# Tables asked for after the first weights, and 144 modulation steps spread anew over two mixers and two gate builds

## The chip, the cores and the metric

The kernel runs on one core of one Trainium2 chip. The metric is the device time of one execution in microseconds; where several executions are told of, it is their median.

## What is computed

Two blocks of a transformer run one after the other on 256 tokens of width 1024, each with two layers. The first block has a mixer and a PEER layer per layer; the second is steered by a condition `c` and has two feed-forward layers and a mixer per layer. Cut to what matters here:

```python
x = x + hgrn_gmlp_mixer(x, ...)          # mix0
x = x + peer_ffn(x, ...)                 # peer0
x = x + mla_moba_mixer(x, ...)           # mix1
x = x + peer_ffn(x, ...)                 # peer1

def peer_ffn(x, norm_ffn, w_query, sub_keys, expert_down, expert_up):
    # top 16 of 128x128 experts for each token and each of 8 heads
    act = gelu(einsum('btd,bthkd->bthk', xi, take(expert_down, idx)))
    return einsum('bthk,bthkd->btd', g * act, take(expert_up, idx))

def adaln(cond, w, b):                   # once per layer of the second block,
    mm = jax.nn.silu(cond) @ w + b       # for c and for c_ctx
    return nine rows of 1024             # w is 1024 x 9216

x = x + 0.5 * m[2] * swiglu(modulate(x, g, m[0], m[1]), ffn1_wi, ffn1_wo)
x = x + m[5] * mixer(modulate(x, g, m[3], m[4]))
x = x + 0.5 * m[8] * swiglu(modulate(x, g, m[6], m[7]), ffn2_wi, ffn2_wo)
```

The modulation (`adaln`) depends on the condition alone. It can be computed at any time before the second block begins.

## The kernel before, in words

Activations lie transposed, 128 features by 256 tokens to a tile. A product with weights is made of three matmuls (`mm3`, lines 170 to 172): weights and activations are each split into a rounded part and a rest (`whi` and `wlo`, `xnh` and `xnl`), and high by high, high by low and low by high are added up. Weights come in units of 512 KB (128x1024, fp32). For each unit SP issues a DMA (`raw`, line 85), ACT casts it (`whi`, line 93), and DVE or POOL subtracts the cast from it (`wlo`, line 97). All stages share three slots for `raw`.

The stages run in this order: `mix0` (`hgrn_gmlp`), `peer0`, `mix1` (`mla_moba`), `peer1`, then the second block. In a mixer, an input projection is followed by the heads' own work (scores at line 408, the gMLP product at line 443, head norms `hps` and `hrb` at lines 287 and 296) and by an output projection into `acc`. A PEER layer begins with a norm (`nps`, line 226) and the routing: 16 units of `l_wq`, each followed by a score product with `keys` (line 530, keys issued at line 513). Then come the *gate build* and the expert products. In the build, one-hot tables for four tokens at a time are made by DVE and ACT, and PE multiplies them into `gps` (line 641), while the down products of the first 46 experts (`dn`) are spread among them. Behind the build come the other downs, with the up products (`acc`).

A *modulation step* (`Mod.step`, line 931) loads 512 KB of `w_mod` (`mraw`, line 937) and multiplies it by the condition in four column-tiled fp32 matmuls (line 942). Eight steps make a row. The eighth copies the row out of PSUM (`mrow`, line 946), two transposes turn it (line 948), and two DVE additions write it away (line 952). There are 72 steps to a layer, 144 in all.

Where the steps stand is set by three numbers and a scheduler. In a mixer they are given out ahead of it under `n.low()`, with a priority far behind the mixer's own work and a pool of their own of three slots. The scheduler puts them into each engine's program where it expects that engine to be free, but none may stay behind when the mixer ends, since the pools close there. In a PEER layer they are given out when the downs reach number 46 (line 670), from the `raw` slots that the weights use. The order in each engine's program is fixed when the kernel is built: 40 steps of layer 0 in the first mixer (`M_0`), 32 of layer 1 in the first build (`N_MOD`), the other 32 of layer 0 in the second mixer (`M_1`), and the last 40 of layer 1 in the second build.

At the start SP issues `vec`, the two halves of `x`, then `ident` and `iota` (lines 119 and 120), then the six tables of the first mixer (line 131), then the first three `raw` and the first three `mraw`.

Of the kernel before, what the change touches and what calls it, by code (L numbers as in the profile page):

```python
# [18 lines left out]
T = 256  # L19
# [2 lines left out]
NEG = -1.0e30  # L22
N_STORE = 40
N_LAG = 16
N_PARK = 3
N_MOD = 32
M_0 = 40
M_1 = 72
PAT_1 = "gggv"
PAT_0 = "gv"  # L30
M_BUFS = 3
# [69 lines left out]
class Net:  # L101
    def __init__(self, ctx, tc, d):
        self.ctx, self.tc, self.nc, self.d = ctx, tc, tc.nc, d
        nc = self.nc
        pool = lambda name, bufs, **k: ctx.enter_context(tc.tile_pool(name=name, bufs=bufs, **k))
        self.cp = pool("const", 1)
        self.main = Stream(self, ctx, "w", 3, 3)
        self.xn_p = None
        self.ps, self.bufs, self.rotation, self.turn = None, {}, [], 0
        self.x = self.cp.tile([128, NDC, T], F32, name="x")  # L110
        self.vec = self.cp.tile([128, NVEC], F32, name="vec")
        self.ident = self.cp.tile([128, 128], F32, name="ident")
        self.ones = self.cp.tile([128, 128], F32, name="ones")
        self.iota = self.cp.tile([128, 128], F32, name="iota")
        self.eps = self.cp.tile([128, 1], F32, name="eps")
        nc.sync.dma_start(out=self.vec, in_=d["vec"])
        for c in range(0, NDC, X_DMA):
            nc.sync.dma_start(out=self.x[:, c:c + X_DMA], in_=d["x_t"][:, c:c + X_DMA])
        nc.sync.dma_start(out=self.ident, in_=d["c_ident"])
        nc.sync.dma_start(out=self.iota, in_=d["c_iota"])  # L120
        nc.vector.memset(self.ones, 1.0)
        nc.vector.memset(self.eps, EPS)
        self.stream = self.main
# [181 lines left out]
def hgrn_gmlp(n: Net):  # L305
    nc, d = n.nc, n.d
    n.rotation = ["mm", "ac", "mm", "ac", "mm", "ac", "ac"]
    n.stream.pattern = PAT_0
    with ExitStack() as st:
        p = st.enter_context(n.tc.tile_pool(name="m0", bufs=1, reuse_waits="tile"))  # L310
        w2 = st.enter_context(n.tc.tile_pool(name="m0w", bufs=2, reuse_waits="tile"))
        xn, rn = n.scaled(n.x, n.v("l0_norm_mix"), None, None, p)
        rc = n.columns(rn, p)
        sel = n.const("c_sel", p, [128, 4, 128])
        lev = n.const("c_lev", p, [128, 6, 128])
        smask = n.const("c_scan", p, [128, T])
        tril = n.const("c_tril", p, [128, 128])
        gws = n.const("gmlp_ws", p, [128, 4, 128])
        gbs = n.const("gmlp_bs", p, [128, 4, 128])


        lb = n.v("lb").rearrange("p (r h) -> p r h", r=3)
# [41 lines left out]
        def tiles(kt, qt, dst):  # L364
# [9 lines left out]
            out=s, in0=ps, in1=n.ident.unsqueeze(1).to_broadcast([128, 4, 128]), op=OP.mult))  # L374
# [110 lines left out]

def peer(n: Net, layer, mod, mod_upto):
    nc, d = n.nc, n.d
    pre = f"l{layer}_"  # L490
    NS = N_STORE
# [1 line left out]
    with ExitStack() as st:  # L493
# [123 lines left out]
        with ExitStack() as sg:  # L617
            gp = sg.enter_context(n.tc.tile_pool(name="gg", bufs=1, reuse_waits="tile"))
            gg = gp.tile([128, 128 - NS, T], F32, name="gg")
            onehot = n.tc.tile_pool(name="oneh", bufs=OH, reuse_waits="tile")  # L620
            o2 = onehot.__enter__()
            for t0 in range(0, T, 4):
                a = o2.tile([128, 4, 128], F32, tag="oa", name="oa")
                b = o2.tile([128, 4, 128], F32, tag="ob", name="ob")
                g = n.bank("gps").rearrange("p (t e) -> p t e", t=4)


                by_act = t0 // 4 * N_ACT % 16 < N_ACT
                nc.vector.tensor_tensor(out=a, in0=n.iota.unsqueeze(1).to_broadcast([128, 4, 128]),
                                        in1=it[:, 0, t0:t0 + 4].unsqueeze(2).to_broadcast([128, 4, 128]),  # L630
                                        op=OP.is_equal)
                for t in range(4):
                    at = lambda s: it[:, s, t0 + t:t0 + t + 1]
                    if by_act:
                        nc.scalar.activation(out=b[:, t], in_=n.iota, func=AF.Abs, scale=-1.0, bias=at(1))
                        nc.scalar.activation(out=b[:, t], in_=b[:, t], func=AF.Relu, scale=-2.0, bias=at(2))
                    else:
                        nc.vector.tensor_scalar(out=b[:, t], in0=n.iota, scalar1=at(1), scalar2=at(2),
                                                op0=OP.is_equal, op1=OP.mult)
                for t in range(4):  # L640
                    nc.tensor.matmul(g[:, t], a[:, t], b[:, t], start=t == 0, stop=True, skip_group_check=True)  # L641
                ge = g.rearrange("p t e -> p e t")
                nc.vector.tensor_tensor(out=ca[:, :, t0:t0 + 4], in0=ca[:, :, t0:t0 + 4], in1=ge[:, 0:NS], op=OP.mult)
                nc.scalar.copy(out=gg[:, :, t0:t0 + 4], in_=ge[:, NS:128])
            n.stream.pattern = PAT_G
            onehot.__exit__(None, None, None)
            g2 = sg.enter_context(n.tc.tile_pool(name="gg2", bufs=2, reuse_waits="tile"))

            def coef(i):
                return ca[:, i] if i < NS else gg[:, i - NS]  # L650

            acc = []

            def up(i):
                if not acc:
                    acc.extend(n.accs())
                w = n.unit(d[pre + "up"][i])
                c = coef(i)
                ch = g2.tile([128, T], F32R, tag="ch", name="ch")
                cl = g2.tile([128, T], F32R, tag="cl", name="cl")  # L660
                n.split(c, ch, cl)
                n.up(acc, w, (ch, cl), i == 0, i == 127)

            done = 0
            for i in range(NS, 128, 2):
                def sink(b):
                    nc.scalar.activation(out=b, in_=b, func=AF.Gelu_apprx_tanh)
                    c = gg[:, i - NS:i - NS + 2]
                    nc.vector.tensor_tensor(out=c, in0=c, in1=b, op=OP.mult)
                if i == NS + 2 * N_PARK:  # L670
                    while mod.next < mod_upto:
                        mod.step(n.main.raw_p)
                    mod.bank = None
                down_pair(i, sink, "ac" if i < NS + 2 * N_PARK else None)
                while i >= NS + 2 * N_PARK and done < i + 2 - N_LAG:
                    up(done)
                    done += 1
            while done < 128:
                up(done)
                done += 1  # L680
            n.residual(n.x, acc)
# [779 lines left out]
def two_blocks_kernel(ctx: ExitStack, tc: tile.TileContext, d, out, stages=None):  # L1461
    stages = stages or STAGES
    n = Net(ctx, tc, d)
    nc = n.nc
# [9 lines left out]
    for s in stages:  # L1474
        with tc.tile_pool(name="xn", bufs=1, reuse_waits="tile") as n.xn_p:
# [4 lines left out]
                    (hgrn_gmlp if s == "mix0" else mla_moba)(n)  # L1480
            elif s.startswith("peer"):
                with n.psum(ac=4, mm=2, m2=2):
                    peer(n, int(s[4]), mods[1], N_MOD if s[4] == "0" else 72)
            elif s.startswith("mod"):
                with n.psum(ac=4, mm=2, fl=2), tc.tile_pool(name="mod", bufs=3, reuse_waits="tile") as p:
                    aside(mods[int(s[3])], p, 72)
# [172 lines left out]
```

## Time and profile before

| what | value |
|---|---|
| median of 3 runs | 3417.71 us (3415.21 to 3419.04) |
| the profiled execution | 3413.94 us |
| its span in the trace | 3412.1 us |
| mean granted clock of TensorE | 0.984 |
| first mixer | 0 to about 190 us |
| first gate build, first score to first up product | 198.2 to 483.4 us |
| second mixer, its last product | ends at 1246.4 us |
| second gate build, likewise | 1256.5 to 1557.7 us |

The span is the time from the first to the last instruction that the profiler recorded; the profiled execution took 1.84 us more. The places in the table are starts of instructions in the trace, in microseconds from the start of the span. What one edit is worth is read at such a place: which engine is waited for there, and what stands behind the wait in its program.

### The profile page before, as it was taken

How to read it: one execution, taken by the hardware profiler on the slowest of the kernel's cores; microseconds unless marked ns; L12 is line 12 of the kernel's file. 1: busy time of each engine (PE TensorE's matmuls, PEld its weight loads, DVE VectorE, ACT ScalarE, POOL GpSimd, SP SyncE). 2: the span in 40 equal slices, each digit the busy share in tenths (PEclk: the TensorE clock that was granted, in tenths of full speed). 3: DMA queues.
4: the chain of work that ended last, by engine and by line, in shares of the span. 5: the costliest groups of instructions: out<-in, count | busy, mean ns of one | idle time of the engine just before them, and what ended most of it. 6: DMA issues, size and time to landing. Idle time of an engine off the chain costs nothing.

```text
span 3412.1 us, 65304 instructions
## 1 busy us (share of the span) xinstructions
PE 3286.0 (96%) x26792; PEld 3139.3 (92%) x26792; DVE 2144.8 (63%) x4167; ACT 1684.6 (49%) x2720; POOL 169.5 (5%) x79
## 2 busy tenths in 40 slices
PE   7999999999999999999999999899999989999898
PEld 6789989999999679978999999899999779999898
DVE  6489785555556559785555555666766656666565
ACT  5444774444445344584544444544644444454543
POOL 2200000000001310000000000200000010100100
PEclk9999999999999999999999999999999889999999
DMA  6645465555555545456655555554454235455453
GB/s 229 231 159 180 150 222 182 202 185 181 184 183 193 193 144 169 161 200 208 201 183 185 182 184 183 202 184 138 155 172 148 77 124 185 168 179 173 143 185 106
DMA packets 165755, 598.28 MB, mean 175 GB/s; under 512 B 18512, under 2 KB 20176, under 8 KB 164944
## 3 DMA queue, kind: packets, MB, share of 16 engines
q1 hardware_dynamic: 165456, 594.11, 52.0%
q8 instruction: 210, 3.44, 0.4%
q14 instruction: 89, 0.73, 0.1%
HBM read 592.99 MB, written 1.05 MB: 174 GB/s over the span
## 4 chain that ended last, share of the span: by engine, by line
PE 86%; DVE 7%; DMA 3%; ACT 2%; issue 1%; SPq 0%; ACTq 0%; DVEq 0%
PE acc L170 11%; PE acc L171 11%; PE acc L172 10%; PE dn L172 7%; PE dn L171 7%; PE dn L170 7%; PE ff L170 6%; PE ff L171 6%; PE ff L172 6%; DMA mraw<-w_mod 2%; PE gps L641 2%; PE mm L170 2%; PE mm L171 2%; PE mm L172 2%; PE mod L942 2%; DVE wlo L97 2%
## 5 line engine op out<-in xcount | busy, mean ns | idle before, releaser
L93 ACT CAST whi<-raw 128x1024 fp32r<-128x1024 f32 x969 | 1014.0, 1048 | 1400.5 <-PE acc L171 533.2
L97 DVE TENSOR_TENSOR wlo<-raw,whi 128x1024 fp32r<-128x1024 f32 x904 | 1110.4, 1229 | 827.9 <-ACT whi L93 827.5
L172 PE MATMUL dn<-xnh,wlo 128*128 128x256 f32 x2048 | 581.2, 284 | 2.9 <-DVE wlo L97 2.9
L170 PE MATMUL dn<-xnh,whi 128*128 128x256 f32 x2048 | 581.1, 284 | 1.2 <-ACT whi L93 1.2
L171 PE MATMUL dn<-xnl,whi 128*128 128x256 f32 x2048 | 580.9, 284 | 0.0
L171 PE MATMUL acc<-cl,whi 128*128 128x256 f32 x2048 | 567.5, 283 | 1.0 <-DVE cl L165 1.0
L172 PE MATMUL acc<-ch,wlo 128*128 128x256 f32 x2048 | 566.4, 283 | 0.0
L170 PE MATMUL acc<-ch,whi 128*128 128x256 f32 x2048 | 533.8, 283 | 0.0
L170 PE MATMUL ff<-xnh,whi 128*128 128x258 f32 x1760 | 503.6, 287 | 12.5 <-DVE x L209 3.9
L171 PE MATMUL ff<-xnl,whi 128*128 128x258 f32 x1760 | 502.5, 286 | 3.7 <-DVE xnl L247 3.7
L172 PE MATMUL ff<-xnh,wlo 128*128 128x258 f32 x1760 | 500.4, 284 | 3.3 <-POOL wlo L97 1.9
L172 PEld LDWEIGHTS dn<-xnh,wlo 128*128 128x128 f32 x2048 | 393.1, 192 | 3.8 <-DVE wlo L97 3.8
L170 PEld LDWEIGHTS dn<-xnh,whi 128*128 128x128 f32 x2048 | 393.7, 192 | 1.6 <-ACT whi L93 1.6
L171 PEld LDWEIGHTS acc<-cl,whi 128*128 128x128 f32 x2048 | 393.2, 192 | 1.4 <-DVE cl L165 1.4
L171 PEld LDWEIGHTS dn<-xnl,whi 128*128 128x128 f32 x2048 | 393.6, 192 | 0.0
L172 PEld LDWEIGHTS acc<-ch,wlo 128*128 128x128 f32 x2048 | 392.7, 192 | 0.0
L170 PEld LDWEIGHTS acc<-ch,whi 128*128 128x128 f32 x2048 | 373.1, 192 | 0.0
L170 PEld LDWEIGHTS ff<-xnh,whi 128*128 128x128 f32 x1760 | 334.8, 191 | 16.7 <-ACT rstd L216 4.8
L171 PEld LDWEIGHTS ff<-xnl,whi 128*128 128x128 f32 x1760 | 336.8, 192 | 5.3 <-DVE xnl L247 4.6
L172 PEld LDWEIGHTS ff<-xnh,wlo 128*128 128x128 f32 x1760 | 335.4, 191 | 4.6 <-POOL wlo L97 2.5
L97 POOL TENSOR_TENSOR wlo<-raw,whi 128x1024 fp32r<-128x1024 f32 (+1 forms) x65 | 156.3, 2411 | 2754.4 <-ACT whi L93 2726.9
L171 PE MATMUL acc<-hl,whi 128*128 128x256 f32 x880 | 246.1, 281 | 3.1 <-DVE hl L1019 3.1
(449 smaller groups left out, 5315.6 us busy)
## 6 DMA issues: line engine op xcount, KB each, us to landing
raw<-l_down SPq DMA_DIRECT2D x256, 512.0 KB, 3.3
raw<-l_up SPq DMA_DIRECT2D x256, 512.0 KB, 4.2
mraw<-w_mod SPq DMA_DIRECT2D x144, 512.0 KB, 4.3
raw<-f1i SPq DMA_DIRECT2D x132, 512.0 KB, 3.3
raw<-f2i SPq DMA_DIRECT2D x88, 512.0 KB, 3.3
raw<-f1o SPq DMA_DIRECT2D x66, 512.0 KB, 3.3
raw<-w_t SPq DMA_DIRECT2D x46, 512.0 KB, 4.3
raw<-f2o SPq DMA_DIRECT2D x44, 512.0 KB, 3.4
```

The lines of the kernel that those rows point to most:

```text
L93: nc.scalar.copy(hi[:, 0:k], raw[:, 0:k])
L97: eng.tensor_tensor(out=low[:, 0:k], in0=raw[:, 0:k], in1=hi.bitcast(F32)[:, 0:k], op=OP.subtract)
L170: mm(out, w[0], x[0], start=first, stop=False, skip_group_check=True)
L171: mm(out, w[0], x[1], start=False, stop=False, skip_group_check=True)
L172: mm(out, w[1], x[0], start=False, stop=last, skip_group_check=True)
L641: nc.tensor.matmul(g[:, t], a[:, t], b[:, t], start=t == 0, stop=True, skip_group_check=True)
L942: nc.tensor.matmul(ps[32 * j:32 * j + 32], n.cond[:, k], raw[:, j * T:(j + 1) * T], start=k == 0, stop=k == NDC - 1, tile_position=(0, 32 ...
```

## The change

The loads of `ident` and `iota` and of the six tables get a priority behind that of the first weights (`low(FIRST)`). The three numbers change: 24 steps of layer 0 in the first mixer, 40 of layer 1 in the first build, 40 of layer 0 in the second mixer, and in the second build the 8 that are left of layer 0 and then 32 of layer 1. So that a build can take steps of two layers, `peer` gets a list of pairs.

```diff
+FIRST = 200
 N_PARK = 3
-N_MOD = 32
-M_0 = 40
-M_1 = 72
+N_MOD = 40
+M_0 = 24
+M_1 = 64
...
-        nc.sync.dma_start(out=self.ident, in_=d["c_ident"])
-        nc.sync.dma_start(out=self.iota, in_=d["c_iota"])
+        with self.low(FIRST):
+            nc.sync.dma_start(out=self.ident, in_=d["c_ident"])
+            nc.sync.dma_start(out=self.iota, in_=d["c_iota"])
...
         xn, rn = n.scaled(n.x, n.v("l0_norm_mix"), None, None, p)
+        with n.low(FIRST):
+            sel = n.const("c_sel", p, [128, 4, 128])
+            lev = n.const("c_lev", p, [128, 6, 128])
+            smask = n.const("c_scan", p, [128, T])
+            tril = n.const("c_tril", p, [128, 128])
+            gws = n.const("gmlp_ws", p, [128, 4, 128])
+            gbs = n.const("gmlp_bs", p, [128, 4, 128])
         rc = n.columns(rn, p)
-        sel = n.const("c_sel", p, [128, 4, 128])
...
-def peer(n: Net, layer, mod, mod_upto):
+def peer(n: Net, layer, mods):
...
                 if i == NS + 2 * N_PARK:
-                    while mod.next < mod_upto:
-                        mod.step(n.main.raw_p)
-                    mod.bank = None
+                    for mod, upto in mods:
+                        mod.tag = "ac"
+                        while mod.next < upto:
+                            mod.step(n.main.raw_p)
+                        mod.bank = None
...
-                    peer(n, int(s[4]), mods[1], N_MOD if s[4] == "0" else 72)
+                    peer(n, int(s[4]), [(mods[1], N_MOD)] if s[4] == "0" else [(mods[0], 72), (mods[1], 72)])
```

Lines move by up to five: the step's load is line 937 before and 942 after, its matmuls 942 and 947, the transposes 948 and 953, the gate product 641 and 644, the norm 226 and 228, and `mm3` stands at 170 to 172 and at 172 to 174.

What that does to the order is shown at three places. The first is SP's program at its start, before and after; `raw` are the first weights, `mraw` the first loads of modulation steps, all between them are tables.

```order
L116 DMA vec<-vec 128x298
L118 DMA x<-x_t 128x1024 x2
L119 DMA ident<-c_ident 128x128
L120 DMA iota<-c_iota 128x128
L131 DMA c_sel<-c_sel 128x512
L131 DMA c_lev<-c_lev 128x768
L131 DMA c_scan<-c_scan 128x256
L131 DMA c_tril<-c_tril 128x128
L131 DMA gmlp_ws<-gmlp_ws 128x512
L131 DMA gmlp_bs<-gmlp_bs 128x512
L85 DMA raw<-w_t 128x1024 x3
L937 DMA mraw<-w_mod 128x1024 x3
```

```order
L117 DMA vec<-vec 128x298
L119 DMA x<-x_t 128x1024 x2
L86 DMA raw<-w_t 128x1024 x3
L121 DMA ident<-c_ident 128x128
L122 DMA iota<-c_iota 128x128
L133 DMA c_sel<-c_sel 128x512
L133 DMA c_lev<-c_lev 128x768
L133 DMA c_scan<-c_scan 128x256
L133 DMA c_tril<-c_tril 128x128
L133 DMA gmlp_ws<-gmlp_ws 128x512
L133 DMA gmlp_bs<-gmlp_bs 128x512
L942 DMA mraw<-w_mod 128x1024 x3
```

The three weights now stand ahead of eight table loads. ACT's program moves with them: the pairs of logarithm-gate operations at lines 347 and 352 stand two and two in place of one and one, with four table loads of ACT (`ACT_TABLE_LOAD`) fewer in this stage.

The second place is PE's program at the end of the first gate build. A step is `mod<-mraw,cond` x4 there, and `dn` are the next down products.

```order
L641 MATMUL gps<-ob,oa 128x128 x4
L942 MATMUL mod<-mraw,cond 32x256 x4
L641 MATMUL gps<-ob,oa 128x128 x4
L942 MATMUL mod<-mraw,cond 32x256 x4
L641 MATMUL gps<-ob,oa 128x128 x11
L948 MATMUL mod<-ident,mrow 128x128 x2
L641 MATMUL gps<-ob,oa 128x128 x5
L170 MATMUL dn<-xnh,whi 128x256
```

```order
L644 MATMUL gps<-ob,oa 128x128 x4
L947 MATMUL mod<-mraw,cond 32x256 x4
L644 MATMUL gps<-ob,oa 128x128 x4
L947 MATMUL mod<-mraw,cond 32x256 x4
L644 MATMUL gps<-ob,oa 128x128 x11
L953 MATMUL mod<-ident,mrow 128x128 x2
L644 MATMUL gps<-ob,oa 128x128 x5
L947 MATMUL mod<-mraw,cond 32x256 x32
L953 MATMUL mod<-ident,mrow 128x128 x2
L172 MATMUL dn<-xnh,whi 128x256
```

Thirty-two steps stand among the gate products as before; the eight new ones stand in one piece behind the last gate product and ahead of the next down product. The second build had such a piece of eight steps before, and has it still. From the downs of the second PEER layer on, the order is that of before.

The third place is the end of the second mixer. PE's program after the change goes from the last output product (`acc`) to the norm of the second PEER layer (`nps`) as follows; before, `nps` stood directly behind the last `acc` product.

```order
L172 MATMUL acc_13559<-yh,whi 128x256
L173 MATMUL acc_13559<-yl,whi 128x256
L174 MATMUL acc_13559<-yh,wlo 128x256
L947 MATMUL mod<-mraw,cond 32x256 x32
L953 MATMUL mod<-ident,mrow 128x128 x2
L228 MATMUL nps<-sq,ones 128x256 x2
L172 MATMUL mm<-xnh,whi 128x256
```

SP's program of the same place, before and after:

```order
L937 DMA mraw<-w_mod 128x1024 x3
L85 DMA raw<-l_wq 128x1024
L937 DMA mraw<-w_mod 128x1024 x2
L85 DMA raw<-l_wq 128x1024 x3
L513 DMA keys<-l_keys 128x2048
L85 DMA raw<-l_wq 128x1024 x11
```

```order
L942 DMA mraw<-w_mod 128x1024
L86 DMA raw<-l_wq 128x1024
L942 DMA mraw<-w_mod 128x1024 x2
L86 DMA raw<-l_wq 128x1024
L516 DMA keys<-l_keys 128x2048
L942 DMA mraw<-w_mod 128x1024 x3
L86 DMA raw<-l_wq 128x1024
L942 DMA mraw<-w_mod 128x1024 x2
L86 DMA raw<-l_wq 128x1024 x10
```

Eight steps now stand between the last output product and the norm, and five of their loads stand behind the load of `keys`, which is 1 MB. At the end of the first mixer it is the other way about: three steps, the two transposes and the additions stood between the last `acc` product and `nps`, and after the change `nps` follows directly. Inside the first mixer, 16 steps stand ahead of the scores of line 408 in both programs; behind them stood 24, and now stand 8.

## Rows read from the trace of the kernel before

**Rows 1.** The page's first part: busy time, share of the span, instructions of each engine.
```profile
PE 3286.0 (96%) x26792; PEld 3139.3 (92%) x26792; DVE 2144.8 (63%) x4167; ACT 1684.6 (49%) x2720; POOL 169.5 (5%) x79
```

**Rows 2.** Stretches: length, then busy time of each engine, granted clock, DMA share, GB/s.
```profile
84.00:190.00 106.00, 94.24 (x804) 80.71 (x803) 47.10 (x88) 47.32 (x71) 23.99 (x10) 0.98 0.70 238
10.00:20.00 10.00, 8.57 (x45) 6.23 (x46) 5.12 (x6) 7.96 (x12) 3.81 (x2) 1.00 0.99 375
1535.00:1550.00 15.00, 7.79 (x67) 1.88 (x68) 3.93 (x11) 2.29 (x5) 0.00 (x0) 0.66 0.81 272
```

**Rows 3.** Waits of PE in 84 to 190 us: total us, times, longest.
```profile
PE mod L942 <- DMA mraw<-w_mod: 4.7, 4, 2.7
```

**Rows 4.** ACT's timeline at the front: start, us, engine, line, operation, [idle before].
```profile
9.84 0.70 ACT L225 ACTIVATE sq<-x 128x256 f32<-128x256 f32 x2
...
13.14 1.04 ACT L93 CAST whi<-raw 128x1024 fp32r<-128x1024 f32 x1 [0.33 <-DMA raw<-w_t]
...
17.06 0.48 ACT L216 ACTIVATE rstd<-nps,eps 128x256 f32<-128x256 f32 x1
...
33.44 1.28 ACT L347 ACT_TABLE_LOAD   x1
34.73 0.42 ACT L347 ACTIVATE lf<-lf 128x256 f32<-128x256 f32 x1
...
43.89 1.03 ACT L93 CAST whi<-raw 128x1024 fp32r<-128x1024 f32 x1
```

**Rows 5.** POOL's timeline at the front: its first weight split.
```profile
14.27 2.36 POOL L97 TENSOR_TENSOR wlo<-raw,whi 128x1024 fp32r<-128x1024 f32 x1 [13.83 <-ACT whi L93]
```

**Rows 6.** PE's timeline at the front: two products of the first weight.
```profile
16.91 0.28 PE L170 MATMUL mm<-xnh,whi 128*128 128x256 f32 x1
...
17.97 0.28 PE L170 MATMUL mm<-xnh,whi 128*128 128x256 f32 x1
```

**Rows 7.** PE's timeline, second half of the first mixer.
```profile
108.61 1.49 PE L942 MATMUL mod<-mraw,cond 128*32 128x256 f32 x20
...
161.17 0.64 PE L942 MATMUL mod<-mraw,cond 128*32 128x256 f32 x8 [1.12 <-DMA mraw<-w_mod]
...
164.72 1.97 PE L296 MATMUL hrb<-hr,c_sel 128*128 128x256 f32 x8 [1.62 <-DVE hr L217]
...
176.57 1.06 PE L942 MATMUL mod<-mraw,cond 128*32 128x256 f32 x12
```

**Rows 8.** PE's timeline, end of the first mixer and first score of the first PEER layer.
```profile
182.75 0.28 PE L172 MATMUL acc<-yh,wlo 128*128 128x256 f32 x1
...
187.09 0.44 PE L948 MATMUL mod<-ident,mrow 128*128 128x128 f32 x2 [1.60 <-DVE mrow L946]
189.70 2.04 PE L226 MATMUL nps<-sq,ones 128*128 128x256 f32 x4 [2.18 <-DVE mod L952]
...
198.22 0.71 PE L530 MATMUL mm<-keys,qt 128*128 128x128 f32 x4 [0.43 <-ACT qt L542]
```

**Rows 9.** PE's timeline: first up product behind the first build, and behind the second.
```profile
483.41 0.64 PE L170 MATMUL acc<-ch,whi 128*128 128x256 f32 x4
...
1557.70 0.28 PE L170 MATMUL acc<-ch,whi 128*128 128x256 f32 x1
```

**Rows 10.** PE's timeline, behind the last gate product of the second build.
```profile
1538.09 0.64 PE L942 MATMUL mod<-mraw,cond 128*32 128x256 f32 x8 [1.89 <-DMA mraw<-w_mod]
...
1546.23 1.08 PE L942 MATMUL mod<-mraw,cond 128*32 128x256 f32 x8 [0.83 <-DMA mraw<-w_mod]
1547.86 0.69 PE L948 MATMUL mod<-ident,mrow 128*128 128x128 f32 x2 [0.55 <-DVE mrow L946]
```

**Rows 11.** PE's timeline, end of the second mixer and first score of the second PEER layer.
```profile
1246.08 0.28 PE L172 MATMUL acc<-yh,wlo 128*128 128x256 f32 x1
...
1256.48 0.71 PE L530 MATMUL mm<-keys,qt 128*128 128x128 f32 x4 [0.42 <-ACT qt L542]
```

**Rows 12.** DMA issues in 1245 to 1252 us: count, KB each, median us to landing.
```profile
keys<-l_keys SPq DMA_DIRECT2D x1, 1024.0 KB, 5.6
```

More of the change, by code (lines that the diff above doesn't have):

```diff
@@ L312, in hgrn_gmlp @@
         xn, rn = n.scaled(n.x, n.v("l0_norm_mix"), None, None, p)
-        rc = n.columns(rn, p)
-        sel = n.const("c_sel", p, [128, 4, 128])
[L315 to L319, printed above, removed]
+        with n.low(FIRST):
[5 more added lines that the diff above has]
+            gbs = n.const("gmlp_bs", p, [128, 4, 128])
+        rc = n.columns(rn, p)
         lb = n.v("lb").rearrange("p (r h) -> p r h", r=3)
```

## The prediction

> **What bounds the kernel now.** I read the page's first part first: PE is busy for 96% of the span [rows 1]. So a microsecond of PE work that is taken off or added counts in full unless PE waited there anyway. Then the stretches: in the second half of the first mixer PE is busy for 94.2 of 106 us, DMA is at 70%, and no other engine is half busy [rows 2]. Behind the second gate build it is the other way about: PE is busy for 7.8 of 15 us, DMA is at 0.81, and the granted clock is 0.66 [rows 2]. There the modulation steps stand alone, and PE waits for their loads. So a step has two prices. Among other work it costs PE's own time. Alone, in a piece, it costs the time of a 512 KB load. The waits say the same: in the first mixer's second half PE waited for `mraw` only four times, 4.7 us in all [rows 3], while behind the second build nearly every step has such a wait [rows 10]. The change moves 16 steps out of the first mixer and puts eight behind the first build and eight behind the second mixer, each time in one piece with nothing beside it in PE's program.
>
> **(a) The front of the first mixer: -3.3 us.** The first weights are issued ahead of eight tables. The first cast starts at 13.14, released by its load [rows 4]. With the load earlier it can follow the squares that end at 10.5 (9.84 + 0.70), a gain of 2.6 on that cast. It does not carry through. In the new order the last norm products stand behind the products of the first weights, and the weight's low part comes from POOL, whose split takes 2.36 us [rows 5]: 10.5 + 1.04 + 2.36 = 13.9. Some 39 products at 0.118 us each (1.06 us for nine, from 16.91 to 17.97 [rows 6]) are 4.6, and three norm products about 1.4 more, so the root that starts at 17.06 [rows 4] starts at 19.9. What ACT has behind it then gets shorter: from the root to the end of the cast at 43.89 are 27.9 us now (44.92 - 17.06). Out of these go one cast that is made ahead (1.04) and four table loads of 1.28 (5.1), which leaves 21.7, and 19.9 + 21.7 = 41.6 against 44.92. Bounds: 0, if PE and not ACT sets the pace there, and -7.7, if both gains arrive (2.6 + 5.1).
>
> Here a rule prices the table loads otherwise. The row: a load starts at 33.44, takes 1.28, and the logarithm behind it starts at 34.73 [rows 4], so there is nothing but the load. The Trainium skill ("ScalarE: Activation LUTs", section "What ACT_TABLE_LOAD costs") has the same 1283 ns and adds a drain of some 1380 ns to every switch. By the page four switches would be about 10.6 us and (a) -8.8 (an estimate); the trace doesn't show a drain there, so the sum goes by the row.
>
> **(b) The rest of the first mixer: -8.4 us.** Of the 16 steps taken out (24 to 8 behind the scores) some 13 are on PE's path; the others stood in a wait that stays. A piece of 12 matmul records takes 1.06 us and one of 20 takes 1.49 [rows 7], so the eight records of a step cost 0.43 (0.45 with the gap): 13 times this is 5.9. At the head norms two steps hold PE up for a load (1.12 us [rows 7]) and for their own time (twice 0.4), and behind them `hrb` stands waiting for what DVE makes of the norms: -1.9. Two rows fewer to finish, partly in waits: -0.6. Bounds: -3, if only the steps in full stretches count, and -11.9, if all 16 steps (7.2) and all 4.7 us of waits [rows 3] go.
>
> **(c) The end of the first mixer: -5.1 us.** Now the last output product ends at 183.03 (182.75 + 0.28), then three steps run, the transposes wait for `mrow` until 187.09, the norm waits for the additions until 189.70, and the first score starts at 198.22 [rows 8]: 15.2 us. At the second mixer's end, where no step stands in this place, it is from 1246.36 to 1256.48 [rows 11]: 10.1. After the change the first mixer's end has that form. The two ends agree to the microsecond in what follows the norm, so I allow 1 us either way.
>
> **(d) The end of the first build: +16.0 us.** The order puts eight steps behind the last gate product, exactly as in the second build, which had 40 steps before. So the price is the difference between the two builds of the same kernel. From the first score to the first up product they take 285.2 us (198.22 [rows 8] to 483.41 [rows 9]) with 32 steps and 301.2 (1256.48 [rows 11] to 1557.70 [rows 9]) with 40. The piece shows why: step follows step at 1.63 us (1538.09 to 1546.23 is five [rows 10]) where the matmuls take 0.64 to 1.08. Nothing covers it: the next downs stand behind it in PE's program, and their weights want the same three slots. Bounds: 13 (eight at 1.63) and 17.
>
> **(e) The end of the second mixer: +14.3 us.** The trace of before has no such piece ahead of a norm, so I build it up. Let T be the last output product's end, 1246.36. Three steps have their loads by then and run at once. The other five loads stand in SP's program behind `keys`, and wait for the slots of the first three. `keys` lands 5.6 us after its issue [rows 12], about T + 5.3. Behind it come five steps and a unit of `l_wq`, six times 512 KB. At the 375 GB/s that the queue reached when it was full (10 to 20 us [rows 2]) one takes 1.40 us, together 8.4, so T + 13.7. Then the last matmuls (0.45), the wait for `mrow` (0.55) and the transposes (0.69) [rows 10], and the additions (about 0.6): the norm starts at T + 16.0. From the norm to the first score it was 8.5 at the first mixer's end (189.70 to 198.22 [rows 8]): T + 24.4 against T + 10.1. Bounds: 8.3, if five loads are early (5.1 as in (c), and five times 0.64), and 17.4, if it runs at the second build's pace (16.0) with an `l_wq` unit between (1.4).
>
> **The sum.** -3.3 - 8.4 - 5.1 + 16.0 + 14.3 = +13.5 us. Everything behind the second PEER layer's first downs stands as before and is costed at nothing. The profiled execution took 3413.94 us, 3.8 under the median of 3417.71; against these the sum gives 3427.4 and 3431.2. I take **3430 us**. About 0.2% (6.8 us) is what a measurement of this kernel can tell from no change.
>
> **Rivals.** *One piece is covered* (same, about 3415). If one of the two pieces turns out to go under work that runs anyway, 16.0 falls out and -2.5 is left. The loads are independent of all else, and DMA is far from full over most of the span. Against it: before the change the same piece of eight in the second build was not covered, and cost PE half its time there [rows 2]. The Trainium skill ("Perfetto Trace Analysis", section "Optimization Strategy") says that a kernel whose busiest engine changes over time may gain by interleaving such regimes. That would hold of the steps here if they stood among PE's products; by the order of the change they don't. 0.15.
>
> *The first mixer's steps cost more than their matmuls* (faster, about 3408). This is the other side. If each of the 16 gives back what a step in a piece costs (2.0 us, 16.0 by 8) in place of 0.45, because their loads held up the mixer's weights in the queue, (b) is -32 and the sum -3.3 - 32 - 5.1 + 30.3 = -10.1. The sign turns at about 1.4 us a step, and beyond 1.8 it is faster by over 0.2%. For it: DMA is at 70% there, more than in the builds. Against it: PE waited for `mraw` for 4.7 us only and was busy for 94 of 106 [rows 2, 3], so there are not 32 us to give back. 0.07.
>
> *The front gains nothing and both pieces cost their upper bounds* (slower, 3438 to 3443): 0 - 8.4 - 5.1 + 17 + 17.4 = +20.9 with the clock as it is, and some 4 us more if it stays low behind each pause of PE as it did behind the second build (0.66 [rows 2]). 0.09.
>
> That the change doesn't do what it says is excluded by the order: the steps stand where the numbers put them.
>
> **How the numbers follow.** The forecast has 0.69. Its own spread takes in the bounds: (e) 6 us down and 3 up, (b) 3.5 down and 5.4 up, (a) 4.4 down and 3.3 up; they are independent of each other, so about 8 us either way, and 0.03 of it lies under +6.8. With the rivals: faster 0.07, same 0.15 + 0.03 = 0.18, slower 0.66 + 0.09 = 0.75. The range reaches from 3416, the upper part of the covered case, to 3440, within the worst case.
>
> **What would show it.** Right: in the first build eight steps behind the last gate product, most with a wait for `mraw`, and about 301 us from the first score to the first up product; behind the second mixer some 24 us from the last output product to the first score, with the last `mraw` landing at about 14; the first mixer's first score at about 181; the second build unchanged; four table loads of ACT fewer at the front. Wrong: a first score much earlier than 178 (the second rival), no waits for `mraw` in one of the two pieces (the first), or a front in which the cast now at 43.89 is not earlier.

## The result

The changed kernel is slower. Its median was 3438.4 us beside 3417.6 of the kernel before in the larger comparison (6 executions against 23), a ratio of 1.0062 (95% interval 1.0046 to 1.0077); in the first comparison the ratio was 1.0058 (1.0043 to 1.0074). One execution of the changed kernel in the first comparison took 15697.8 us and is left out of that ratio. The larger comparison gives +16 to +26 us on 3417.7, or some 3439 where 3430 was forecast and 3416 to 3440 was the range. The sign was right and the size was too small by a third.

The profiled execution of the changed kernel took 3445.3 us with a span of 3443.4, and so shows more (+31) than the median does. A second profile of the same program had a span of 3435.7. Stages that no edit touches differ by several microseconds between profiles, so the reading below goes by stages and not by spans.

The page's first part, after, beside [rows 1]:

```profile
PE 3300.5 (96%) x26792; PEld 3148.2 (91%) x26792; DVE 2150.0 (62%) x4167; ACT 1679.6 (49%) x2716; POOL 172.5 (5%) x79
```

PE was busy 14.5 us longer with the same 26792 instructions. How much of that is the change is not shown: in the second profile of the changed kernel PE is busy for 3294.4 us, and for 3294.5 in the profile of e1_front below, whose steps stand as before and whose time is that of before. ACT has 4 instructions fewer, the table loads.

This table is worked out from PE's timelines, as differences of starts and ends, in microseconds; each row is one profile, and "after, again" is the second profile of the changed kernel (e1_after_again below). "To scores" is the front up to line 408 of the kernel before; "to acc" goes from there to the last output product of the first mixer; "end 0" and "end 1" go from the last output product of a mixer to the first score of the PEER layer; "build" goes from that score to the last gate product, and "behind" from there to the first up product.

| kernel | to scores | to acc | end 0 | build 0 | behind 0 | end 1 | build 1 | behind 1 |
|---|---|---|---|---|---|---|---|---|
| before | 83.2 | 99.8 | 15.2 | 278.6 | 6.6 | 10.1 | 278.5 | 22.7 |
| after | 86.0 | 93.7 | 9.0 | 280.2 | 24.0 | 26.0 | 280.8 | 24.5 |
| after, again | 87.9 | 94.5 | 9.0 | 277.9 | 24.8 | 27.4 | 278.1 | 23.3 |
| e1_front | 85.9 | 102.9 | 11.1 | 279.6 | 6.6 | 10.6 | 280.6 | 23.2 |
| e1_counts | 86.1 | 92.8 | 9.8 | 281.8 | 24.5 | 27.0 | 277.7 | 23.2 |
| e1_swap | 82.7 | 98.0 | 15.4 | 280.3 | 23.9 | 10.7 | 281.5 | 6.3 |
| e2_front_dve | 80.5 | 96.6 | 22.6 | 279.9 | 6.5 | 9.2 | 279.3 | 23.7 |
| e2_double | 83.2 | 101.4 | 15.5 | 280.5 | 40.5 | 12.5 | 284.6 | 3.7 |
| e2_weave8 | 84.8 | 99.7 | 15.1 | 278.0 | 6.5 | 10.3 | 330.1 | 5.8 |
| e2_weave | 83.1 | 91.1 | 9.0 | 327.9 | 6.5 | 10.3 | 344.9 | 5.8 |
| e3_weave_late | 85.5 | 100.7 | 15.5 | 280.4 | 6.6 | 9.9 | 287.0 | 12.8 |
| e3_no_piece | 84.2 | 98.1 | 9.6 | 291.3 | 13.7 | 10.3 | 287.7 | 12.8 |
| e3_no_piece_dve | 80.6 | 92.6 | 9.6 | 291.0 | 12.3 | 9.5 | 285.6 | 12.5 |
| e3_dve_alone | 79.9 | 95.0 | 21.5 | 279.0 | 6.6 | 11.8 | 279.8 | 23.0 |

Behind the first build the changed kernel has this on PE (timeline; the rows of the second build before were [rows 10]):

```profile
468.74 1.07 PE L947 MATMUL mod<-mraw,cond 128*32 128x256 f32 x16
472.01 0.98 PE L947 MATMUL mod<-mraw,cond 128*32 128x256 f32 x8 [2.20 <-DMA mraw<-w_mod]
...
478.87 1.08 PE L947 MATMUL mod<-mraw,cond 128*32 128x256 f32 x8 [0.40 <-DMA mraw<-w_mod]
480.51 1.08 PE L947 MATMUL mod<-mraw,cond 128*32 128x256 f32 x8 [0.56 <-DMA mraw<-w_mod]
482.14 0.69 PE L953 MATMUL mod<-ident,mrow 128*128 128x128 f32 x2 [0.55 <-DVE mrow L951]
484.32 0.58 PE L172 MATMUL dn<-xnh,whi 128*128 128x256 f32 x1 [1.48 <-ACT whi L94]
...
492.80 0.28 PE L172 MATMUL acc<-ch,whi 128*128 128x256 f32 x1
```

Two steps run at once, then each waits for its load; the next down product waits for its cast, because its weight was loaded after the steps. The six loads that PE waits for here land 4.0 to 5.0 us after their issue, and they are issued as steps leave the three slots. A slot's round of 4.3 us (the median) for the load and 1.08 for the step, by three, is 1.8 us a step (an estimate from these rows), near the 1.63 to 2.1 that the pieces of these kernels show. DMA is at 0.77 over the piece, so not full. A kernel with more slots was not run, so whether they set the price is argued and not shown.

Behind the second mixer, on PE and on SP (beside [rows 11]):

```profile
1255.87 0.28 PE L174 MATMUL acc<-yh,wlo 128*128 128x256 f32 x1
1256.08 1.07 PE L947 MATMUL mod<-mraw,cond 128*32 128x256 f32 x16
1257.88 0.64 PE L947 MATMUL mod<-mraw,cond 128*32 128x256 f32 x8 [0.73 <-DMA mraw<-w_mod]
1265.09 1.08 PE L947 MATMUL mod<-mraw,cond 128*32 128x256 f32 x8 [6.57 <-DMA mraw<-w_mod]
...
1270.57 1.08 PE L947 MATMUL mod<-mraw,cond 128*32 128x256 f32 x8 [1.85 <-DMA mraw<-w_mod]
1271.84 1.08 PE L947 MATMUL mod<-mraw,cond 128*32 128x256 f32 x8 [0.18 <-DMA mraw<-w_mod]
...
1274.58 2.04 PE L228 MATMUL nps<-sq,ones 128*128 128x256 f32 x4 [0.42 <-DVE mod L964]
...
1282.17 0.71 PE L533 MATMUL mm<-keys,qt 128*128 128x128 f32 x4 [0.43 <-ACT qt L545]
```

```profile
1255.88 0.43 SPq L516 DMA_DIRECT2D keys<-l_keys  x1
1256.78 3.44 SPq L942 DMA_DIRECT2D mraw<-w_mod  x3
1260.31 0.51 SPq L86 DMA_DIRECT2D raw<-l_wq  x1
1266.23 1.62 SPq L942 DMA_DIRECT2D mraw<-w_mod  x2
```

The load of `keys`, from its issue to its landing (beside [rows 12]):

```profile
keys<-l_keys SPq DMA_DIRECT2D x1, 1024.0 KB, 7.9
```

Three steps run, the fourth waits 6.57 us for a load issued behind `keys`, and the last two loads are issued from 1266.23 on, when the fourth step has left its slot. The stretches of both pieces, as in [rows 2] (length, busy time of PE, PEld, DVE, ACT and POOL, granted clock, DMA share, GB/s):

```profile
1256.00:1274.00 18.00, 7.72 (x68) 1.87 (x66) 6.85 (x17) 4.86 (x11) 0.00 (x0) 0.63 0.74 272
468.80:483.00 14.20, 8.09 (x67) 1.80 (x66) 3.43 (x9) 1.26 (x4) 0.00 (x0) 0.62 0.77 258
```

PE is about half idle, and the mean granted clock is 0.62 and 0.63: part of each piece runs at the lower level of 1.2 GHz, where eight records take 1.08 us in place of 0.64. In the first build the granted clock was 1.00 from 468.80 to 471.50 and 0.51 from 472 to 483, after PE had stood 2.20 us for a load.

### The profile page after: what moved, and what is told of

Its sections match the earlier page's. It is cut to its first block, busy times and chain, and to the rows that moved or that the text cites. A ratio compares the mean times of both kernels' runs of the same rounds, so it can differ in the third digit from the quotient of the medians.

```text
span 3443.4 us, 65301 instructions
## 1 busy us (share of the span) xinstructions
PE 3300.5 (96%) x26792; PEld 3148.2 (91%) x26792; DVE 2150.0 (62%) x4167; ACT 1679.6 (49%) x2716; POOL 172.5 (5%) x79
## 4 chain that ended last, share of the span: by engine, by line
PE 84%; DVE 8%; DMA 4%; ACT 3%; issue 1%; SPq 0%; ACTq 0%; DVEq 0%
PE acc L172 10%; PE acc L173 10%; PE acc L174 10%; PE dn L174 7%; PE dn L173 7%; PE dn L172 7%; PE ff L172 6%; PE ff L173 6%; PE ff L174 6%; DMA mraw<-w_mod 3%; PE gps L644 2%; DVE wlo L98 2%; PE mm L172 2%; PE mm L173 2%; PE mm L174 2%; PE mod L947 2%
```

## The experiments

The theory after the result (A): a step in a piece costs the time of its load, the two pieces cost 16 to 18 us each, the first mixer gives back 12 or so, and the front gives nothing. The first four kernels take the change apart.

**e1_after_again**: no edit.

> The changed kernel as it is, for a second profile of it. In its first profile the second build, whose order did not change, took 305.3 us from first score to first up product, where the kernel before took 301.2. Theory A (a matter of the run): this profile shows about 301 to 302 there, and a span some 4 to 10 us shorter than 3443.4. Theory B (a cost of the change that reaches into the second PEER layer): 305 again. Both expect about 26 us from the last output product of the second mixer to the first score, and about 24 us from the last gate product of the first build to the first up product.

Measured: 1.0062 (1.0046 to 1.0077), span 3435.7. The second build took 301.4 us (278.1 + 23.3), as in the kernel before. So the 305 of the first profile was a matter of the run; the builds without woven steps differ by 4 us between the profiles of these kernels (277.7 to 281.8; only the second build of e2_double, which has 24 steps, took 284.6). Both pieces came out as in the first profile.

**e1_front**: the hunks on `FIRST` alone.

```diff
+FIRST = 200
 N_MOD = 32
 M_0 = 40
 M_1 = 72
```

> The table loads behind the first weights, all counts of steps as before. By the prediction's term (a): 3.3 us faster than before, with the scores of line 408 about 3.3 earlier than 83.2. Theory A, from the changed kernel's first profile: it gains nothing, because the root of the norm comes 3.3 later, the fourth weight comes late, and DVE's weight splits run beside POOL's; scores at about 86, total 0 to +4. Four ACT table loads fewer under both.

Measured: 1.0001 (0.9990 to 1.0011), scores at 85.9. Term (a) is not there. The first weight is cast 3 us earlier, and then it is lost; ACT's timeline of the changed kernel, beside [rows 4]:

```profile
10.13 1.03 ACT L94 CAST whi<-raw 128x1024 fp32r<-128x1024 f32 x1
...
20.41 0.48 ACT L218 ACTIVATE rstd<-nps,eps 128x256 f32<-128x256 f32 x1 [1.54 <-PE nps L228]
22.06 1.04 ACT L94 CAST whi<-raw 128x1024 fp32r<-128x1024 f32 x1 [1.17 <-DMA raw<-w_t]
23.34 1.05 ACT L94 CAST whi<-raw 128x1024 fp32r<-128x1024 f32 x1 [0.24 <-DMA raw<-w_t]
...
43.14 1.03 ACT L94 CAST whi<-raw 128x1024 fp32r<-128x1024 f32 x1
```

The fourth weight's cast starts at 22.06, where it started at 22.12 before. The queue explains that. SP's rows for the next weights, after and then before:

```profile
13.69 3.60 SPq L86 DMA_DIRECT2D raw<-w_t  x3
```

```profile
16.66 4.64 SPq L85 DMA_DIRECT2D raw<-w_t  x3
```

The fourth weight is issued 3.0 us earlier and lands 8.3 us after its issue in place of 4.7, so at about 22.0 in place of 21.4. Stretches of the front, after and then before:

```profile
3.00:12.00 9.00, 3.80 (x9) 2.42 (x10) 4.63 (x18) 8.93 (x18) 0.76 (x1) 1.00 1.00 357
12.00:24.00 12.00, 11.90 (x92) 9.77 (x91) 7.42 (x4) 6.28 (x10) 4.80 (x2) 1.00 0.96 349
```

```profile
3.00:12.00 9.00, 3.79 (x8) 2.30 (x8) 5.34 (x19) 7.83 (x17) 0.00 (x0) 1.00 1.01 359
12.00:24.00 12.00, 10.85 (x74) 8.75 (x74) 5.95 (x9) 10.48 (x14) 4.75 (x2) 1.00 0.91 330
```

The DMA engines are all but full in both (0.91 to 1.01). The change permutes the bytes; by the fourth weight the same tables and weights have to be through. That the scores then came 2.7 us later than before does not follow from the queue, and is within what one program shows at this place (e1_counts).

**e1_counts**: the change with `FIRST = 0`, which leaves SP's start as it was.

> The counts of steps as changed (24, 40, 40, 8 + 32), the tables ahead of the first weights as before. By the prediction's terms (b) to (e): +16.8 against before. Theory A: both pieces of eight steps cost what the first profile shows (19.0 and 15.9), the first mixer gives back some 12, so +20 to +25; scores of line 408 at about 83. If the front is what made the changed kernel slower than forecast, this one comes out about 3 us under the changed kernel.

Measured: 1.0057 (1.0042 to 1.0072), so the counts are the whole effect, as far as the runs can tell. Both +16.8 and +20 lie in this interval. Its program up to the scores is that of the kernel before, yet the scores came at 86.1 and not at 83.2: one step, at 71.9 in the trace before, stood 2.2 us longer for its load, and the 16 products behind the steps there took 3.58 us in place of 2.02. So 3 us at this place tell nothing by themselves.

**e1_swap**: one number.

```diff
-N_MOD = 32
+N_MOD = 40
```

> Only the number of steps in the first build is raised to 40; the second build then has 32 and both mixers are as before. So the piece of eight moves from behind the second build to behind the first. Theory A (a piece costs the same in either build): +16 to +19 in the first build, -16 to -18 in the second, total within 3 us of before. Rival (the second build hides its piece, or the first one does): total +16 or -16. From first score to first up product: about 302 and about 285 where before had 285 and 301.

Measured: 1.0006 (0.9996 to 1.0016). The piece went from one build to the other (behind 0: 6.6 to 23.9; behind 1: 22.7 to 6.3), and the total stayed. A piece of eight costs 16 to 18 in either.

**e2_front_dve**: e1_front, and

```diff
-PAT_0 = "gv"
+PAT_0 = "v"
```

In the trace of the changed kernel two DVE operations were long beside a split on POOL:

```profile
35.49 2.55 DVE L303 TENSOR_TENSOR_SCAN bb<-c_scan,lf 128x256 f32<-128x256 f32 x1
...
41.62 3.38 DVE L98 TENSOR_TENSOR wlo<-raw,whi 128x1024 fp32r<-128x1024 f32 x1
```

```profile
35.11 2.38 POOL L98 TENSOR_TENSOR wlo<-raw,whi 128x1024 fp32r<-128x1024 f32 x1 [8.23 <-ACT whi L94]
...
41.41 2.51 POOL L98 TENSOR_TENSOR wlo<-raw,whi 128x1024 fp32r<-128x1024 f32 x1 [3.92 <-ACT whi L94]
```

> As e1_front (tables behind the first weights, old counts), but in the first mixer every weight split is made by DVE and none by POOL. Theory A (the new order of the front loses its gain because a scan and a split on DVE run while POOL splits, and take 2.5 and 3.4 us where they took 0.7 and 1.2): no DVE split or scan over 2 us in the first 50 us, and the cast that ended at 44.9 before, and the scores of line 408, 2 to 5 us earlier than in e1_front (85.9), unless DVE, which gets 1.2 us more for each of some 10 splits, becomes the engine that PE waits for. Rival (the late loads hold the front up, not DVE beside POOL): scores at 85 to 87 again.

Measured: 0.9986 (0.9974 to 0.9998), scores at 80.5, 5.4 before e1_front's. The scan took 0.69 and that split 1.22:

```profile
35.05 0.69 DVE L303 TENSOR_TENSOR_SCAN bb<-c_scan,lf 128x256 f32<-128x256 f32 x1 [0.98 <-ACT lf L355]
...
43.41 1.22 DVE L98 TENSOR_TENSOR wlo<-raw,whi 128x1024 fp32r<-128x1024 f32 x1
```

A split at 44.87 still took 2.19, beside another operation on POOL (line 397, from 43.51), so "no split over 2 us" was wrong by one. At the mixer's end 7 us were given back (end 0 is 22.6): six steps stand behind the last output product there, where the kernel before had three. Up to the first score of the PEER layer this profile took 199.7 us, e1_front's 199.9 and that of before 198.2, so the 0.14% is not seen in the first mixer, and where it comes from is not shown. Whether the order of the tables had any part in the gain is left to e3_dve_alone.

**e2_double**: `N_MOD = 48` in the kernel before.

> 48 steps in the first build and 24 in the second, mixers as before: the piece behind the first build is 16 steps long, and the second build has none. Theory A (in a piece a step costs the time of its load, about 2.0 to 2.2 us): 6.5 + 34 to 36 = 41 us from the last gate product of the first build to the first up product, 6.5 in the second, total +14 to +19. Rival (the pause behind the build is mostly its ends, the first load and the finishing of the row): some 29 us for 16 steps, total +3 to +7.

Measured: 1.0044 (1.0029 to 1.0060), +15 us, as theory A had it. Sixteen steps cost 34.0 us (40.5 - 6.5) where eight cost 17.4 in e1_swap (23.9 - 6.5). The second eight cost as much as the first, 16.6 and 17.4, so it is a price per step, of 2.1 us, and not one of the ends:

```profile
494.82 1.08 PE L942 MATMUL mod<-mraw,cond 128*32 128x256 f32 x8 [0.80 <-DMA mraw<-w_mod]
...
508.30 1.08 PE L942 MATMUL mod<-mraw,cond 128*32 128x256 f32 x8 [0.54 <-DMA mraw<-w_mod]
```

The steps of the second eight follow each other at 1.93 us (13.5 by 7). Behind the second build 3.7 us were left, and the build before it was 6 us longer; the two together are 3 us over the 285 of a build with 32 steps.

**e2_weave8** and **e2_weave**: a step is given out behind each pair of early down products.

```diff
             for i in range(0, NS, 2):
                 down_pair(...)
+                mod, upto = woven
+                if mod.next < upto:
+                    mod.tag = "mm"
+                    mod.step(n.main.raw_p)
+            woven[0].bank = None
...
-    peer(n, int(s[4]), [(mods[1], N_MOD)] if s[4] == "0" else [(mods[0], 72), (mods[1], 72)])
+    peer(n, int(s[4]), [(mods[1], N_MOD)] if s[4] == "0" else [(mods[1], 72)],
+         (mods[1], 0) if s[4] == "0" else (mods[1], 40))
```

e2_weave has `M_0 = 24`, `M_1 = 56`, `N_MOD = 40`, and weaves 8 steps of layer 1 into the first layer's downs and 16 of layer 0 into the second's.

> Counts and front as before, but of the 40 steps of the second PEER layer the first eight are given out one behind each pair of the first down products, so that they stand among PE's products, and none stands behind the gate build. Theory A (a step among other products costs its matmuls, 0.43 to 0.5 us, in a piece 2.0): 6.5 us from the last gate product to the first up product in place of 22.7, some 4 us more before it, total -10 to -14. Rival (the loads cost their time wherever they stand, since the weights want the same three slots): total -2 to +2.

> No piece anywhere: 24 steps in the first mixer, 8 woven into the downs and 32 in the build of the first PEER layer, 32 in the second mixer, 16 woven and 32 in the build of the second PEER layer; front as before. Theory A: the first mixer gives back 8 to 12 as in e1_counts, the second build's piece 16, and 24 woven steps cost 10 to 12, so -12 to -18 against before. Rival (as in e2_weave8): -4 to +8.

Measured: 1.0094 (1.0077 to 1.0110) and 1.0227 (1.0213 to 1.0241). Both are far slower, more than either theory said. No piece is left behind the build (5.8 us), but the build with woven steps took 328 to 345 in place of 279. In e2_weave8 PE stood here:

```profile
1355.82 0.69 PE L612 MATMUL tp<-ident,key 128*128 128x128 f32 x2 [20.20 <-DVE key L607]
1356.44 2.79 PE L952 MATMUL mod<-mraw,cond 128*32 128x256 f32 x24
```

The transposes of the routing's result stood behind 144 down products in PE's program, not behind 556 as before, and PE stood 20 us for DVE there. With the steps among the downs the order is another one, and what used to cover DVE's routing came after it. So these runs test an order, and not the price of a step. The build of e2_weave8 is 52 us longer than that of before. In 31 of these PE stands idle, 20 at the transpose and 7 more in waits of `dn` for a cast. In the other 21 PE is busy, some 3.5 with the eight steps; its mean granted clock was 0.93 over this build and 1.00 over that of before.

**e3_weave_late**: e2_weave8 with two lines changed.

```diff
-                if mod.next < upto:
-                    mod.tag = "mm"
+                if i >= 24 and mod.next < upto:
+                    mod.tag = "ac"
```

> As e2_weave8 (eight of the second PEER layer's steps one behind each pair of down products), but from the twelfth pair on, with accumulator banks for the steps; 556 down products stand ahead of the first transpose of the routing's result, as many as in the kernel before, where e2_weave8 had 144. Theory A (e2_weave8 lost its gain to PE standing at that transpose for 20 us, and to score banks that DVE still read, not to the loads): no such wait over 2 us, build about 4 to 8 us longer than the 278.5 of before, 6 us from its last gate product to the first up product in place of 22.7, total -8 to -13. Rival (the loads cost their time wherever they stand): build some 16 us longer, total -2 to +3.

Measured: 0.9989 (0.9975 to 1.0003), not to be told from no change; the expectation of -8 to -13 was missed. The wait at the transpose is gone, and 556 products stand ahead of it again. Two lines were changed together, so which of them moved the order back is not shown. The build grew by 6.6 us against the same run's first build (287.0 and 280.4), 0.8 a step, or by 8.5 against that of before, and behind it 12.8 are left, not 6:

```profile
1547.72 0.64 PE L952 MATMUL mod<-mraw,cond 128*32 128x256 f32 x8 [0.16 <-DMA mraw<-w_mod]
1548.90 0.44 PE L958 MATMUL mod<-ident,mrow 128*128 128x128 f32 x2 [0.55 <-DVE mrow L956]
1551.26 0.58 PE L172 MATMUL dn<-xnh,whi 128*128 128x256 f32 x1 [1.92 <-ACT whi L94]
1552.72 0.58 PE L174 MATMUL dn<-xnh,wlo 128*128 128x256 f32 x1 [0.66 <-DVE wlo L98]
```

The last step and the finish of its row stand directly ahead of the next downs, and these wait for their casts and splits. In e2_weave8, where gate products stand between, only 5.8 were left. So neither theory holds as it was put: a woven step cost 0.8 to 1.1 us here, about twice its matmuls, and where the last row is finished at the build's very end, 6 us more are lost there.

**e3_no_piece**: `M_0 = 32`, `M_1 = 64`, `N_MOD = 40`, woven as in e3_weave_late in both layers (8 steps of layer 1, then 8 of layer 0).

> No piece anywhere, woven as in e3_weave_late: 32 steps in the first mixer, 8 woven and 32 in the first build, 32 in the second mixer, 8 woven and 32 in the second build. Theory A: the first mixer gives back 5 to 8 (its end as in e1_counts), the second build's piece 16, 16 woven steps cost 8 to 14: -8 to -16. Rival: +3 to +12.

Measured: 1.0013 (0.9996 to 1.0029), +4 us with an interval of -1 to +10: theory A is out, and the middle lies in the rival's range. End 0 fell to 9.6, as expected. The first build paid 12.7 us for the eight steps woven into it and the second 9.2, so 1.2 to 1.6 a step, and 6 to 7 were paid behind each.

**e3_no_piece_dve** is e3_no_piece with `FIRST = 200` and `PAT_0 = "v"`; **e3_dve_alone** is the kernel before with `PAT_0 = "v"` alone.

> e3_no_piece with the tables behind the first weights and all weight splits of the first mixer on DVE, as in e2_front_dve. Theory A: the two gains add up, some 4 to 8 us under e3_no_piece, since the first mixer's end, which grew by 7 us in e2_front_dve, holds no steps here. Rival (what e2_front_dve gained was a better place for steps of the first mixer): the same as e3_no_piece.

> The kernel before with one change: all weight splits of the first mixer on DVE, none on POOL; the tables stay ahead of the first weights. Theory A (the order of the tables gains some 3 us once POOL is out of DVE's way): scores of line 408 at 82 to 84, 2 to 4 us later than in e2_front_dve (80.5). Rival (taking POOL off the splits is the whole gain): scores at about 80.5, total as e2_front_dve (-4.5).

Measured: 0.9972 (0.9960 to 0.9984) and 0.9977 (0.9964 to 0.9990). e3_dve_alone has the scores at 79.9, with the tables in front: the order of the tables gains nothing even with POOL out of the way, so my theory on the front fell, and its rival stands. Both kernels beat the kernel before and the changed one. Their intervals overlap, so the change of `PAT_0` alone is as good as the runs can tell; the spread of steps shortens end 0 from 21.5 to 9.6, and gives it back in the builds. Against e3_no_piece the gain was larger than theory A had it: 15 us (3408.7 and 3423.4) in place of 4 to 8, and 9 of it stand up to the first score (182.8 and 191.9). For e3_dve_alone the place of the gain is not shown: it reaches the first score at 196.4, and the kernels with 40 steps and POOL's splits do so between 196.1 and 201.7. ACT also has two table loads fewer in it (2718 instructions), which no run separates from the splits.

## Why the prediction was right in sign and too small

- **(a) The front, -3.3: wrong, it gave 0** (e1_front 1.0001). The step that failed is "what ACT has behind it then gets shorter": 41.6 was forecast for the end of the cast that ended at 44.92, and it ended at 44.17 (43.14 + 1.03). The root was foreseen (19.9, measured 20.41), and ACT's work behind it did get shorter, by the 6.2 us of one cast and four table loads. What was left out are ACT's waits: from the root to that cast it waited 2.8 us, where it had waited 0.7 before. For the next two weights it waited 1.4 (1.17 at 22.06, 0.24 at 23.34), and for DVE 1.4. That the queue was full stood in [rows 2] (0.99 from 10 to 20 us). The bound of 0 was the right value, and for the part that the rows show its reason was ACT's waits, not PE's pace. By the drain that the Trainium skill ("ScalarE: Activation LUTs", section "What ACT_TABLE_LOAD costs") adds to a load the miss would have been 5.5 us larger (an estimate). The trace shows no drain here either: a load starts at 24.41, takes 1.28, and the activation behind it starts at 25.70.
- **(b) The first mixer, -8.4: right.** From the scores to the last output product the profiles with 24 steps took 91.1 to 94.5, those with 40 and POOL's splits 98.0 to 102.9 (means 93.0 and 100.4): -7.4. Its parts came out otherwise. In this stretch PE's time in steps fell by 8.8 us (14.5 to 5.7), where 5.9 was forecast for them. The 1.9 at the head norms are not there: `hrb` starts 4.7 us after the first head norm product in place of 5.3, and then takes 3.2 in place of 2.0: its granted clock was 0.59 there, after PE had stood 3.05 us for DVE, and 1.00 before, after 1.62. All four kernels with 24 steps show this (3.2 to 3.6 us), and of those with 40 e2_front_dve (3.4). The second rival, which needed -32 here, is out.
- **(c) The first mixer's end, -5.1: right**, -6.2 in the profile (15.2 to 9.0) and -5.4 between the means of the same two groups (14.6 and 9.2).
- **(d) Behind the first build, +16.0: right in mechanism, 1.4 to 2.2 short**: 24.0 and 24.8 less 6.6. The kernel before's second build was the quickest of all such pieces (22.7, where the others have 23.0 to 24.8), and I took it as it stood. The bound of 17 was too tight. The first rival (a piece is covered) is out, by e1_swap above all.
- **(e) Behind the second mixer, +14.3: right in mechanism, 1.6 to 3 short** (15.9 and 17.3 more than the 10.1 of before; from T to the first score 26.0 and 27.4, against 24.4). The last load landed at T + 15.7 and not at 13.7. The term that was mis-sized is the queue behind `keys`: it took 7.9 us to land, not the 5.6 of [rows 12], since a step's load and a weight lay ahead of it. The 8.4 us from there to the last landing came out at 8.0, and partly by luck: they were worked out from a full queue, but the last two loads waited for a slot. From the norm to the first score it was 7.6 and not 8.5.
- **The first score.** The prediction names it as a sign: about 181. It came at 188.6 and, in the second profile, at 191.4, so this sign failed. The kernels with 24 steps and POOL's splits reach it at 188.0 on average (183.2 to 191.4), those with 40 at 199.3 (196.1 to 201.7): -11.3, where (a), (b) and (c) give -16.8. Of the 5.5 that are missing (a) is 3.3, (b) 1.0, and 1.6 is that the kernels with 24 steps came to the scores later (85.8 and 84.2), which is less than programs that are the same up to there differ by; (c) gave 0.3 more.
- **The sum.** With -11.3 up to the first score, +17.8 and +16.6 for the pieces, it is +23, against +21 measured (0.0062 times 3417.7, +16 to +26). So the forecast was short by (a) with 3.3, (e) with 2.3, (d) with 1.8 and (b) with 1.0, nearly all to the same side, where the prediction let them spread as independent. The 3438.4 of the larger comparison lie just within the end of the range, 3440, which was taken from the worst case.
- **The third rival** (front nothing, both pieces at their upper bounds, 3438 to 3443, chance 0.09) is the one that came nearest. I had put its parts as mishaps. For the front the reason stood in the rows: the queue was full over that stretch (0.99), and there the new order of the issues gained nothing. For the pieces it was the slots and the queue behind `keys`; DMA was at 0.74 and 0.77 there, not full.

## What to carry to other kernels

Read a moved step's price at the place where it will stand, and not where it stood: here it was some 0.45 us in the first mixer, 0.8 to 1.6 woven into the builds, and 2.1 in a piece alone. Before an issue order is changed, look whether the queue is already full over the stretch: here the first weight was cast 3 us earlier, and the fourth no earlier. And after a change to the order, look at what stands ahead of each cross-engine wait: weaving eight steps in made a build 52 us longer (the kernel 33), 20 of them in one wait, where some 400 matmuls that had covered a DVE chain had moved behind it.

## What was not expected of the hardware

DVE operations were stretched by a POOL split that ran beside them: a scan took 2.55 us in place of 0.69, and a split 3.38 in place of 1.20. They ended 0.55 and 1.08 us after the POOL split (38.04 and 37.49, 45.00 and 43.92), so nearly their usual length after it. Not every DVE operation is: two `qq` products, which read a matmul's result, took 0.74 together from 42.35 in the trace of before, beside a POOL split from 42.15 to 44.69. It was not POOL's splits alone: the split of 2.19 us in e2_front_dve ran beside another POOL operation. Taking POOL's share of the splits away and giving DVE more work made the kernel 0.23% faster (0.9977, 0.9964 to 0.9990). Which part of that is the stretching and which is POOL's 2.4 us for a split that DVE does in 1.2 was not taken apart, and of the 7 us the profile shows only 1.8 up to the first score (196.4 and 198.2).

Programs that are the same up to a place reached it 3 us apart (83.2 and 86.1 at the scores), mostly by one load that a step stood for. A stage time of a single profile therefore says little below 3 us, and the readings that rest on less are those that several kernels share: with POOL's splits the scores came at 82.7 to 87.9 in eleven profiles, without them at 79.9 to 80.6 in three.
